# Sparse attention of a two-block network on one core: indexer and values first, selection cut by cost, heads of the first two query blocks as one unit, scores on half of the rows

## The chip, the core and the metric

The kernel runs on one core of a Trainium2 chip. The engines that matter are TensorE (PE in the profile; PEld is its weight load), VectorE (DVE), ScalarE (ACT), GpSimd (POOL) and SyncE (SP, which only issues DMAs here). The metric is the time of one execution on the device in microseconds (us). Before the change three runs took 2680.2, 2684.87 and 2683.86 us, with a median of 2683.86 us.

## What is computed

The network takes 512 tokens of one sequence through two blocks with fp32 weights. The change lies in the sparse attention of the second block. Cut to what matters:

```python
proj = h @ w_in                              # q 1024, k 256, v 256, qi 512, ki 64, wi 8 columns
q, k = _rope(_rmsnorm(q, ...)), _rope(_rmsnorm(k, ...))     # 16 heads, 4 key heads, 64 wide
qi, ki = _rope(qi), _rope(_layernorm(ki, ...))              # 8 index heads, one index key, 64 wide
wi = wi * (IDX_HEADS ** -0.5 * IDX_DIM ** -0.5)
topk = min(TOPK_MAX, T // 4)                 # 128 of 512 tokens
for each block of 128 queries:
    s = jnp.einsum('bqhd,bsd->bqhs', qib, ki)
    score = jnp.einsum('bqhs,bqh->bqs', jax.nn.relu(s), wib)
    score = jnp.where(causal, score, -jnp.inf)
    _, sel = lax.top_k(score, topk)
    logits = jnp.einsum('bqgrd,bqkgd->bqgrk', qg, kg) * scale   # only the selected, causal keys
    p = jax.nn.softmax(logits, axis=-1)
    o = jnp.einsum('bqgrk,bqkgd->bqgrd', p, vg)
return o @ w_out
```

## The kernel before

Activations lie transposed (features on partitions, 512 tokens on columns). A projection with fp32 weights is three products of a weight split in two parts: `whi` (a rounded copy that ACT makes, L124) and `wlo` (the rest, L126, a subtraction on DVE, or on POOL where `W.pool_lo` is set: every second one at True, all of them at 2). L461, L462 and L463 are those products. `one_T` computes one tile of 128 output features in 24 matmuls; behind each tile `proj_T` calls `step()`, which runs the closures in `deferred` and then one portion of the generator in `side_work`.

`dsa_block` works in this order: index projections (`ki`, then four tiles `QI`), two k tiles, eight q tiles, two v tiles, and then the attention. Index scores: `score()` (L1557) multiplies a QI tile, which holds two heads on the upper and lower 64 partitions, by `kiA` or `kiB`, copies of `ki` whose other 64 partitions are zero (POOL memsets, L1484 and L1485). ACT takes the relu (L1565) and DVE adds up the heads with their weights (L1567, L1569) into one row of scores for each query. Selection of block j: 16 rounds on DVE, each a search for the eight largest (`max`, L1589) and their replacement by a mark (`match_replace`, L1591), and then the mask `sel[j]` (`taken`, L1602). Block 0 has no more than 128 keys and takes the causal mask. The generator `select()` runs beside the k, q and v tiles: index scores a few heads at a time, rounds for blocks 1 and 2 by the table `PLAN`, then those for block 3.

The norm of q needs sums of squares: one L1628 matmul for each q tile adds to 20 rows in PSUM, and `sums_out` and `roots` make the factors `rq` from them once.

The attention is a loop over 32 units (j, hp), a unit being two heads of one query block: first blocks 1 and 2 in turn, then blocks 3 and 0 in turn. `scores(u)`: two matmuls L1730 against `KZ`, zero-padded copies of k; DVE masks, scales and takes the extreme in one instruction for each head (L1738); ACT takes the exponential with its row sum (L364). `divided(u)`, one unit later: reciprocal on DVE (L1746) and two POOL multiplications (L1748). `transposed(u)`, three units later: L1757 and two ACT copies (L1760). `values(u)`, five units later: L1770, with the two heads on the two halves of the columns, and a split of the result on ACT and DVE (L1774, L1775) for the output projection (L544).

What sets the order is the code itself: every engine takes its instructions in the order in which they are written.

Of the kernel before, what the change touches and what calls it, by code (L numbers as in the profile page):

```python
# [10 lines left out]
F32 = mybir.dt.float32  # L11
# [7 lines left out]
P = 128  # L19
# [218 lines left out]
def body(ctx: ExitStack, tc: tile.TileContext, A: dict, consts: bass.AP, out: bass.AP,  # L238
# [75 lines left out]
    mhalf = cp.tile([P, 4], F32, tag="mhalf", name="mhalf")  # L314
# [1138 lines left out]
    def dsa_block(layer):  # L1453
# [27 lines left out]
        kiA, kiB = big("U4"), big("U5")  # L1481
        KZ = [(big(f"U{6 + 2 * g}"), big(f"U{7 + 2 * g}")) for g in range(4)]
        def zeros(a, b):
            nc.gpsimd.memset(a[64:128], 0.0)  # L1484
            nc.gpsimd.memset(b[0:64], 0.0)  # L1485

        def evac_qi(c, ps):
            raw = tmp()
            nc.scalar.copy(raw, ps)
            rope(QI[c], raw)  # L1490
            zeros(*KZ[c])
# [4 lines left out]
        def evac_ki(c, ps):  # L1496
            raw = big("F4")
            nc.scalar.copy(raw[0:72], ps[0:72])
            zeros(kiA, kiB)
            x = raw[0:64]  # L1500

            def rest():
# [11 lines left out]
                def more():  # L1514
# [10 lines left out]
                    def last():  # L1525
                        nc.scalar.copy(kiA[0:64], x)
                        nc.scalar.copy(kiB[64:128], x)
# [18 lines left out]
        def score(*heads):  # L1546
# [3 lines left out]
            for j, h in heads:  # L1550
# [25 lines left out]
        PLAN = ((6, 0), (6, 0), (4, 4), (0, 4), (0, 4), (0, 4))  # L1576
        to_score = [(j, h) for j in (1, 2, 3) for h in (0, 2, 4, 6)]

        def select():

            def some_scores():
                if ready and to_score:
                    score(*[to_score.pop(0) for _ in range(min(2, len(to_score)))])

            def rounds(j, n):
                sc = marks[j][:, 0:P * (j + 1)]
                for _ in range(n):
                    m8 = colt((P, 8))
                    nc.vector.max(m8, sc)  # L1589
                    yield  # L1590
                    nc.vector.match_replace(sc, m8, sc, TAKEN)  # L1591
                    yield

            def some_rounds(*many):
                todo = [rounds(*x) for x in many if x[1]]
                while todo:
                    todo = [x for x in todo if next(x, True) is None]

            def taken(j):
                sel[j] = sel_t[:, j - 1] if j < 3 else sel_u[:, 0]  # L1600
                n = P * (j + 1)
                nc.vector.tensor_scalar(sel[j][:, 0:n], marks[j][:, 0:n], -2e38, NEG, op0=ALU.is_gt, op1=ALU.mult)  # L1602

            while len(to_score) > 8:
                some_scores()
                yield
            for n1, n2 in PLAN:
                some_rounds((1, n1), (2, n2))
                yield
                some_scores()  # L1610
            taken(1)
            taken(2)
            for _ in range(16):
                some_rounds((3, 1))
                yield
            taken(3)
# [5 lines left out]

        def squares(t, ps, start, stop):
            sq = side("acc", (P, S))
            nc.scalar.activation(sq, ps, AF.Square)

            def add():
                nc.tensor.matmul(ss[0:20, 0:S] if t >= 2 else ss[0:20, S:2 * S], zsel[:, t, :], sq,  # L1628
                                 start=start, stop=stop)

            deferred.append(add)

        kraw = [big("F5"), big("F0")]

        def evac_k(c, ps):
            nc.scalar.activation(kraw[c], ps, AF.Copy, scale=cB[:, 73:74])
            squares(c, ps, c == 0, c == 1)
            if c == 0:
                return

            def rest():
                v, y = tmp()[0:4], sp1.tile([P, 768], F32, tag="wide", name=nm("wide"))[0:4, 0:S]
                nc.vector.tensor_scalar(v, ss[0:4, S:2 * S], 1.0 / 64, EPS, op0=ALU.mult, op1=ALU.add)
# [4 lines left out]
                def copies(g):  # L1648
                    (a, b), o = KZ[g], kraw[g // 2][64 * (g % 2):64 * (g % 2) + 64]
                    nc.scalar.copy(a[0:64], o)  # L1650
                    nc.scalar.copy(b[64:128], o)
                    if g < 3:
                        deferred.append(lambda: copies(g + 1))

                def more():
                    for t in range(2):
                        p1 = pm()

                        nc.tensor.matmul(p1, kexp[t], y, start=True, stop=True)
                        o, z = kraw[t], side("ada_w", (P, 768))[:, 0:S]  # L1660
                        nc.vector.tensor_tensor(z, o, p1, op=ALU.mult)
                        rope(o, z, then=(lambda: copies(0)) if t else None)
# [270 lines left out]
```

## Time and profile before

| | us | busy share of the span |
|---|---|---|
| median of three runs | 2683.86 | |
| profiled execution | 2684.03 | |
| its span | 2682.3 | |
| PE busy | 2635.3 | 98% |
| DVE busy | 1385.7 | 52% |
| ACT busy | 918.2 | 34% |
| POOL busy | 541.9 | 20% |

The span is the time between the first and the last instruction of the profiled execution; 1.7 us lie around it. Busy shares are means over all stages. A stage is read by four views: the busy time in a stretch, the chain of work that ended last, the instructions of one engine in order of time with the idle time ahead of each and what ended it, and groups of like instructions with their mean.

### The profile page before, as it was taken

The numbers are of one execution on the slowest core, as the hardware profiler recorded it, in microseconds if no ns is written. First come the engines' busy times: TensorE is split into PE (matmuls) and PEld (weight loads), VectorE is DVE, ScalarE is ACT, GpSimd is POOL, SyncE is SP. The second block draws the span as 40 slices with busy tenths as digits, with TensorE's granted clock in tenths as the row PEclk, the third lists the DMA queues.
The fourth block names the chain that finished last, engine by engine and source line by source line (L and its number), as shares of the span: only waits on it lengthen the run. The fifth ranks groups of instructions, "written<-read, shape, count | busy, mean of one in ns | idle before, by whom it ended". The sixth has DMA issues, their size and how long they took to land.

```text
span 2682.3 us, 32412 instructions
## 1 busy us (share of the span) xinstructions
PE 2635.3 (98%) x12880; PEld 2174.9 (81%) x12880; DVE 1385.7 (52%) x2072; ACT 918.2 (34%) x1482; POOL 541.9 (20%) x548
## 2 busy tenths in 40 slices
PE   8999999999999999999999899999999999999999
PEld 7888889888777788888888766788888888888887
DVE  5545566375627454665555689453333544533332
ACT  4322233322344433423223436532222332322222
POOL 3211234154112211422123445220000200200000
PEclk9999999999999999999999899999999999999999
DMA  6555443223221323246545131032232322232322
GB/s 187 158 180 185 143 146 118 63 71 95 73 69 48 110 83 122 86 154 199 187 152 160 43 101 60 8 104 87 87 110 75 115 94 96 86 98 83 111 85 71
DMA packets 256474, 288.43 MB, mean 108 GB/s; under 512 B 9924, under 2 KB 238836, under 8 KB 256324
## 3 DMA queue, kind: packets, MB, share of 16 engines
q1 hardware_dynamic: 244196, 234.91, 28.0%
q0 software_dynamic: 10496, 50.95, 6.1%
q8 instruction: 101, 1.65, 0.3%
q10 hardware_dynamic: 1632, 0.52, 0.1%
q14 instruction: 49, 0.40, 0.0%
HBM read 278.59 MB, written 4.19 MB: 105 GB/s over the span
## 4 chain that ended last, share of the span: by engine, by line
PE 90%; DVE 7%; ACT 1%; issue 1%; POOL 1%; DMA 0%; SPq 0%; DVEq 0%; ACTq 0%; POOLq 0%
PE mm L461 25%; PE mm L462 25%; PE mm L463 25%; PE mm L544 2%; PE mm L657 1%; PE mm L659 1%; PE mm L658 1%; PE mm L1730 1%; PE B L1136 1%; DVE X L810 1%; DVE L L696 1%; PE mm L1770 1%; PE A L1279 1%; PE B L1302 1%; DVE F L1591 1%
## 5 line engine op out<-in xcount | busy, mean ns | idle before, releaser
L461 PE MATMUL mm<-H,whi 128*128 128x512 f32 (+1 forms) x2360 | 902.3, 382 | 0.0
L462 PE MATMUL mm<-L,whi 128*128 128x512 f32 (+1 forms) x2360 | 893.7, 379 | 1.4 <-DVE L L696 1.4
L463 PE MATMUL mm<-H,wlo 128*128 128x512 f32 (+1 forms) x2360 | 893.4, 379 | 0.9 <-DVE wlo L126 0.9
L126 DVE TENSOR_TENSOR wlo<-raw,whi 128x1024 fp32r<-128x1024 f32 (+3 forms) x431 | 505.9, 1174 | 555.0 <-ACT whi L124 550.8
L124 ACT CAST whi<-raw 128x1024 fp32r<-128x1024 f32 (+3 forms) x460 | 444.6, 968 | 411.4 <-PE mm L462 332.0
L461 PEld LDWEIGHTS mm<-H,whi 128*128 128x128 f32 x2360 | 445.5, 189 | 91.5 <-issue 10.6
L463 PEld LDWEIGHTS mm<-H,wlo 128*128 128x128 f32 x2360 | 445.3, 189 | 84.2 <-DVE wlo L126 1.6
L462 PEld LDWEIGHTS mm<-L,whi 128*128 128x128 f32 x2360 | 445.8, 189 | 83.6 <-DVE L L696 2.2
L461 PE MATMUL mm<-U,whi 128*128 128x512 f32 (+1 forms) x804 | 312.4, 389 | 0.0
L463 PE MATMUL mm<-U,wlo 128*128 128x512 f32 (+1 forms) x804 | 310.8, 387 | 0.0
L462 PE MATMUL mm<-U,whi 128*128 128x512 f32 (+1 forms) x804 | 310.7, 386 | 0.0
L413 POOL TENSOR_TENSOR acc<-acc,sq 128x512 f32<-128x512 f32 (+1 forms) x74 | 91.9, 1241 | 642.4 <-ACT sq L400 641.7
L670 ACT CAST U<-t 128x512 fp32r<-128x512 f32 x104 | 64.6, 621 | 406.9 <-POOL t L759 194.2
L461 PEld LDWEIGHTS mm<-U,whi 128*128 128x128 f32 x804 | 151.0, 188 | 33.5 <-issue 3.3
L463 PEld LDWEIGHTS mm<-U,wlo 128*128 128x128 f32 x804 | 151.0, 188 | 30.8
L462 PEld LDWEIGHTS mm<-U,whi 128*128 128x128 f32 x804 | 151.0, 188 | 30.2
L671 DVE TENSOR_TENSOR U<-t,U 128x512 fp32r<-128x512 f32 x104 | 72.1, 693 | 134.2 <-ACT U L670 134.2
L882 POOL DMA_DIRECT2D ada_w<-in_ada_w_dram x128 | 71.5, 558 | 281.6 <-DVE wide L906 220.5
L906 DVE SCALAR_TENSOR_TENSOR wide<-ada_w,csilu,wide 128x768 f32<-128x768 f32 x112 | 115.3, 1029 | 16.2 <-DMA ada_w<-in_ada_w_dram 16.2
L126 POOL TENSOR_TENSOR wlo<-raw,whi 128x1024 fp32r<-128x1024 f32 (+1 forms) x29 | 69.5, 2398 | 247.2 <-ACT whi L124 245.6
L757 DVE TENSOR_TENSOR t<-t,mm 128x512 f32<-128x512 f32 x88 | 60.3, 685 | 110.9 <-PE mm L463 110.8
L759 POOL TENSOR_TENSOR t<-t,R 128x512 f32<-128x512 f32 x44 | 56.4, 1283 | 218.4 <-DVE t L757 211.2
(386 smaller groups left out, 2791.7 us busy)
## 6 DMA issues: line engine op xcount, KB each, us to landing
ada_w<-in_ada_w_dram POOLq DMA_DIRECT2D x128, 384.0 KB, 3.6
raw<-in_ffn_w_up_dram SPq DMA_DIRECT2D x44, 1024.0 KB
raw<-in_ffn_w_gate_dram SPq DMA_DIRECT2D x43, 1024.0 KB
raw<-in_w_in_dram SPq DMA_DIRECT2D x30, 1024.0 KB
raw<-in_ffn_w_down_dram SPq DMA_DIRECT2D x32, 768.0 KB
raw<-in_ffn_w_down_dram SPq DMA_DIRECT2D x32, 640.0 KB
raw<-in_w_in_dram SPq DMA_DIRECT2D x24, 512.0 KB
raw<-in_conv_w_in_dram SPq DMA_DIRECT2D x12, 1024.0 KB
```

Of the source, the lines that this page charges most:

```text
L124: nc.scalar.copy(hi, raw)
L126: e.tensor_tensor(lo, raw, hi.bitcast(F32), op=ALU.subtract)
L413: (eng or nc.vector).tensor_tensor(self.acc[:, c], self.acc[:, c], sq[:, c], op=ALU.add)
L461: nc.tensor.matmul(ps, whi, hhi, start=start, stop=False)
L462: nc.tensor.matmul(ps, whi, hlo, start=False, stop=False)
L463: nc.tensor.matmul(ps, wlo, hhi, start=False, stop=stop)
L670: nc.scalar.copy(hi, src)
L671: nc.vector.tensor_tensor(lo, src, hi.bitcast(F32), op=ALU.subtract)
L757: nc.vector.tensor_tensor(s, s, ps, op=ALU.mult)
L759: nc.gpsimd.tensor_tensor(s, s, R, op=ALU.mult)
L882: nc.gpsimd.dma_start(loaded[i], A["ada_w_2"][layer, k * P:(k + 1) * P, 768 * cg:768 * (cg + 1)])
L906: nc.vector.scalar_tensor_tensor(acc, w, csilu[:, k:k + 1], acc, op0=ALU.mult, op1=ALU.add)
```

## The change

It touches `dsa_block` (with `plan_dsa`, the order in which weights are loaded, and the width of the constant `mhalf`).

- **Index.** `ki` is copied to both halves of one tile; a matmul of a head reads 64 partitions of `QI` and the same 64 of `ki`, so that the two heads of a tile stand on different halves of TensorE's rows. `kiA`, `kiB` and the memsets go. `score()` uses the tile `A` for every pair. All of block 1's index scores stand in one step.
- **Selection.** One generator takes block 1, 2 and 3 one after the other; `score()` of block j+1 stands between the rounds of block j. `select(much)` takes portions up to a cost.
- **q and k.** The v tiles stand ahead of the q tiles. v's weights are split by `W.pool_lo = True`, not 2. The squares of each q tile are summed by four small matmuls into columns, and `rq` of its two heads is made at once, with a DVE instruction and five POOL instructions. `KD` holds k doubled on both halves of a tile.
- **Units.** Eight units take blocks 0 and 1 of two heads together; they run beside the q tiles as far as these are there. Eight with block 2 and eight with block 3 follow. `divided(u)` is called right behind `scores(u)`. Results of the units beside the q tiles are kept in fp32 and split later.

The core of the diff (`HALF[i]` is rows 64*i to 64*i+64; line numbers of the changed kernel differ by up to some tens):

```diff
@@ plan_dsa
     plan.append(chunk_T("dsa", w, 0, ND, C["k"], 256))
+    plan.append(chunk_T("dsa", w, 0, ND, C["v"], 256))
     plan += [chunk_T("dsa", w, 0, ND, C["q"] + 256 * c, 256) for c in range(4)]
-    plan.append(chunk_T("dsa", w, 0, ND, C["v"], 256))
@@ score
-                    nc.tensor.matmul(ps, QI[h // 2][:, P * j:P * (j + 1)], (kiA, kiB)[i][:, 0:n],
-                                     start=True, stop=True)
+                for o in range(0, n, 256):
+                    for i in range(2):
+                        c = slice(o, min(o + 256, n))
+                        nc.tensor.matmul(parts[i - 2][2][:, c], QI[h // 2][HALF[i], P * j:P * (j + 1)], ki[HALF[i], c],
+                                         start=True, stop=True)
@@ selection
-        PLAN = ((6, 0), (6, 0), (4, 4), (0, 4), (0, 4), (0, 4))
+            for r in range(16):
+                m8 = colt((P, 8))
+                nc.vector.max(m8, sc)
+                nc.vector.match_replace(sc, m8, sc, TAKEN)
+                yield 0.3 + n / 470
+                if following and r % 4 == 1:
+                    score((following, r // 4 * 2))
+                    yield 0.5 + n / 400
...
+            for h in (0, 2, 4, 6):
+                score((1, h))
+                yield 1.0
+            for j in (1, 2, 3):
+                yield from rounds(j, j + 1 if j < 3 else None)
@@ evac_q
-            squares(2 + c, ps, c == 0, c == 7)
+            sq = side("acc", (P, S))
+            nc.scalar.activation(sq, ps, AF.Square)
             rope(Q[c], raw)
+            def add():
+                both = pm()
+                for j in range(NT):
+                    nc.tensor.matmul(both[:, 2 * j:2 * j + 2], sq[:, P * j:P * (j + 1)], zsel[:, 2, 4:6], start=True,
+                                     stop=True)
+                v, y, z = colt((P, 8)), colt((P, 8)), colt((P, 8))
+                nc.vector.tensor_scalar(v, both[:, 0:8], 1.0 / 64, EPS, op0=ALU.mult, op1=ALU.add)
+                nc.gpsimd.tensor_tensor(y, v, mhalf, op=ALU.pow)
...
+                nc.gpsimd.tensor_tensor(z, y, y, op=ALU.mult)
+                nc.gpsimd.tensor_tensor(z, z, v, op=ALU.mult)
+                nc.gpsimd.tensor_scalar(z, z, 0.5 / 8.0, -1.5 / 8.0, op0=ALU.mult, op1=ALU.add)
...
-        W.pool_lo = 2
-        proj_T("dsa", 2, H, evac_v)
@@ units
-        units = [(j, hp) for hp in range(8) for j in (1, 2)] + [(j, hp) for hp in range(8) for j in (3, 0)]
+        units = [((0, 1), hp) for hp in range(8)] + [((2,), hp) for hp in range(8)] + [((3,), hp) for hp in range(8)]
...
+                for c in range(0, n, 256):
+                    w = min(256, n - c)
+                    for i in range(2):
+                        nc.tensor.matmul(pss[i][:, o + c:o + c + w], Q[hp][HALF[i], P * j:P * (j + 1)],
+                                         KD[hp // 2][HALF[i], c:c + w], start=True, stop=True)
...
+        def unit_step(turn, value):
+            if at[2] < at[1] and at[0] - at[2] >= value:
+                values(at[2])
+                at[2] += 1
+            if at[1] < len(units) and at[0] - at[1] >= turn:
+                transposed(at[1])
+                at[1] += 1
+            u = at[0]
             if u < len(units):
-                while sel[units[u][0]] is None:
-                    step()
                 scores(u)
+                divided(u)
+            at[0] += 1
+        def beside_q():
+            while True:
+                u = at[0]
+                if sel[1] is not None and u < 8 and there[0] > u + 2:
+                    unit_step(1, 2)
+                    select(3.0)
+                else:
+                    select(5.5)
+                yield
+        side_work.append(beside_q())
+        W.pool_lo = True
+        proj_T("dsa", 2, H, evac_k)
+        proj_T("dsa", 2, H, evac_v)
+        proj_T("dsa", 8, H, evac_q)
...
+        while at[2] < len(units):
+            if at[0] < len(units):
+                while sel[units[at[0]][0][-1]] is None:
+                    select(2.0)
+            unit_step(3, 5)
...
+            select(1.4)
             step()
```

How the instructions stand now, at three places. First TensorE behind the second k tile (`A` and `mm` are PSUM tiles, the `U` tiles are QI and ki, `whi` and `H` belong to the next projected tile). Before:

```order
L1628 MATMUL B_11369<-acc_11400,dsa_consts 20x512
L1557 MATMUL A_11436<-U_1184_10974,U_1180_10970 128x256
L1557 MATMUL A_11436<-U_1185_10975,U_1180_10970 128x256
L1557 MATMUL mm_11439<-U_1184_10974,U_1181_10971 128x256
L1557 MATMUL mm_11441<-U_1185_10975,U_1181_10971 128x256
L461 MATMUL mm_11474<-H_1149_10885,whi_11317 128x512
```

and of the changed kernel:

```order
L1650 MATMUL B_11354<-acc_11396,dsa_consts 20x512
L1559 MATMUL A_11432<-U_1184_10974,U_1180_10970 128x256 x2
L1559 MATMUL A_11441<-U_1184_10974,U_1181_10971 128x256 x2
L1559 MATMUL A_11450<-U_1184_10974,U_1182_10972 128x256 x2
L1559 MATMUL A_11459<-U_1184_10974,U_1183_10973 128x256 x2
L461 MATMUL mm_11484<-H_1149_10885,whi_11304 128x512
```

The four heads of the last two QI tiles (`U_1182`, `U_1183`), which stood behind the next tile, stand ahead of it, and all pairs write the one tile `A`.

Second DVE at one unit (`t` are the probabilities, `col` the extremes and the row sums, `F` the row of scores under selection). A unit of block 2 before:

```order
L1738 ISA t_12209,col_12210<-mm_12204,U_1227_11367,R_11473 128x384
L1738 ISA col_12210 128x1
L1738 ISA t_12213,col_12214<-mm_12206,U_1227_11367,R_11473 128x384
L1738 ISA col_12214 128x1
L1589 MAX col_12217<-F_1324_11826 128x8
L1591 MATCH_REPLACE F_1324_11826<-col_12217,F_1324_11826 128x512
L1746 RECIPROCAL col_12208<-col_12208 128x2
```

and the first unit of blocks 0 and 1 in the changed kernel, where L1730, L1739, L1584 and L1585 are what L1738, L1746, L1589 and L1591 were:

```order
L1730 ISA t_11940,col_11942<-mm_11934,masks,R_11365 128x128
L1730 ISA col_11942 128x1
L1730 ISA t_11941,col_11942<-mm_11935,masks,R_11365 128x128
L1730 ISA col_11942 128x1
L1730 ISA t_11940,col_11942<-mm_11934,U_1222_11352,R_11365 128x256
L1730 ISA col_11942 128x1
L1730 ISA t_11941,col_11942<-mm_11935,U_1222_11352,R_11365 128x256
L1730 ISA col_11942 128x1
L1739 RECIPROCAL col_11943<-col_11943 128x4
L1584 MAX col_11957<-F_1258_11510 128x8
L1585 MATCH_REPLACE F_1258_11510<-col_11957,F_1258_11510 128x384
```

The round that stood between a unit's last reduction and its reciprocal stands behind the reciprocal.

Third POOL beside one q tile (`U` is the q tile that is rotated, `ada_w` its raw copy, `t` the swapped halves, `wlo` the low part of a weight). Before:

```order
L1466 TENSOR_TENSOR U_1249_11467<-ada_w_11940,rc_8270 128x512
L126 TENSOR_TENSOR wlo_11951<-raw_11536,whi_11950 128x1024
L1469 TENSOR_TENSOR t_11944<-t_11944,rs_8271 128x512
L1466 TENSOR_TENSOR U_1250_11468<-ada_w_11996,rc_8270 128x512
L1469 TENSOR_TENSOR t_12000<-t_12000,rs_8271 128x512
```

and of the changed kernel:

```order
L1675 TENSOR_TENSOR col_11926<-col_11925,mhalf 128x8
L1677 TENSOR_TENSOR col_11927<-col_11926 128x8
L1678 TENSOR_TENSOR col_11927<-col_11927,col_11925 128x8
L1679 TENSOR_SCALAR col_11927<-col_11927 128x8
L1680 TENSOR_TENSOR R_11365<-col_11927,col_11926 128x4x2
L1741 TENSOR_SCALAR t_11940<-t_11940,col_11943 128x128
L1741 TENSOR_SCALAR t_11941<-t_11941,col_11943 128x128
L1741 TENSOR_SCALAR t_11940<-t_11940,col_11943 128x256
L1741 TENSOR_SCALAR t_11941<-t_11941,col_11943 128x256
L1466 TENSOR_TENSOR U_1230_11360<-ada_w_11974,rc_8270 128x512
L126 TENSOR_TENSOR wlo_11985<-raw_11551,whi_11984 128x1024
L1469 TENSOR_TENSOR t_11978<-t_11978,rs_8271 128x512
```

Between two rotations POOL now has the five instructions of `rq` and the four multiplications of a unit.

## Rows read from the trace of the kernel before

**Rows 1.** Busy time of the engines in four stretches of the sparse attention: start and end, length, then the busy time (and instructions) of PE, PEld, DVE, ACT and POOL, TensorE's granted clock, the DMA engines' share and GB/s. The first stretch holds the k, q and v tiles but for the last; the last ends where the output projection begins.

```profile
1531.80:1630.40 98.60, 91.36 (x333) 59.65 (x332) 82.42 (x156) 42.59 (x71) 51.66 (x38) 0.97 0.36 107
1630.40:1649.30 18.90, 16.16 (x89) 10.36 (x87) 17.79 (x61) 13.01 (x42) 7.49 (x11) 0.91 0.18 57
1649.30:1671.40 22.10, 22.06 (x158) 14.46 (x160) 19.24 (x73) 17.59 (x63) 9.76 (x18) 1.00 0.00 1
1671.40:1717.30 45.90, 45.84 (x373) 30.75 (x373) 23.92 (x106) 36.69 (x128) 18.82 (x36) 1.00 0.01 2
```

**Rows 2.** The chain of work that ended last, in order of time (start, length, engine, tile and line, instructions), where it passes from DVE to PE, in a unit of block 2, in units of block 3, and at the start of the output projection.

```profile
1648.33 0.76 DVE F L1591 x2
...
1649.34 1.56 PE mm L1730 x4
1650.90 0.81 PE mm L1770 x12
1651.70 0.81 PE B L1757 x6
...
1673.01 1.72 PE mm L1730 x4
...
1689.58 1.02 PE mm L1770 x16
1690.60 1.03 PE A L1757 x8
...
1717.30 0.43 PE mm L544 x2
```

**Rows 3.** DVE in order of time: start, length, line, operation, tile and shape, and in brackets the idle time before it with what ended it. The start of the selection; a unit of block 1 and its neighbours in the stretch beside block 3's rounds; a unit of block 2; the mask of block 3.

```profile
1552.55 2.81 DVE L1569 SCALAR_TENSOR_TENSOR F<-sq,wcol,F 128x256 f32<-128x256 f32 x4 [2.96 <-ACT sq L1565]
1556.70 1.39 DVE L126 TENSOR_TENSOR wlo<-raw,whi 128x1024 fp32r<-128x1024 f32 x1 [1.33 <-ACT whi L124]
1558.01 0.41 DVE L1589 MAX8 col<-F 128x8 f32<-128x256 f32 x1
...
1634.36 0.47 DVE L1738 CUSTOM_DVE_ANT_0 acc<-mm,U,R 128x256 f32<-128x256 f32 x1
...
1635.16 0.69 DVE L1589 MAX8 col<-F 128x8 f32<-128x512 f32 x1
...
1636.55 0.15 DVE L1746 RECIPROCAL col<-col 128x2 f32<-128x2 f32 x1
1636.63 0.60 DVE L1738 CUSTOM_DVE_ANT_0 t<-mm,U,R 128x384 f32<-128x384 f32 x1
...
1637.83 0.69 DVE L1589 MAX8 col<-F 128x8 f32<-128x512 f32 x1
...
1656.65 0.28 DVE L1775 TENSOR_TENSOR L<-mm,H 128x128 fp32r<-128x128 f32 x1
1656.84 0.16 DVE L1746 RECIPROCAL col<-col 128x2 f32<-128x2 f32 x1
...
1657.98 0.08 DVE L1738 DVE_READ_ACCUMULATOR2_ANT col<- 128x1 f32 x1
...
1665.62 0.42 DVE L1602 TENSOR_SCALAR U<-F 128x512 bf16<-128x512 f32 x1
```

**Rows 4.** The reductions of block 0's units over the whole span, one group of like instructions (count, busy us, mean ns of one, idle time before them).

```profile
L1738 DVE CUSTOM_DVE_ANT_0 t<-mm,masks,R 128x128 f32<-128x128 f32 x16 | 5.3, 347 | 0.1
```

**Rows 5.** ACT in order of time: the exponentials of the unit of block 2 whose second reduction is read out at 1657.98 us in rows 3; the last row is the read of the second row sum.

```profile
1657.64 0.61 ACT L364 ACTIVATE t<-t,col 128x384 f32<-128x384 f32 x1 [0.81 <-DVE col L1738]
...
1658.76 0.19 ACT L364 ACTIVATION_READ_ACCUMULATOR t<-t,col 128x1 f32 x1
```

**Rows 6.** PE in order of time. First, from an earlier stage, two matmuls with a contraction over four rows, L1257 on rows 0 to 3 of the array and L1258 on rows 32 to 35; then the four scores of a unit of block 1 and the first products with the values behind them.

```profile
757.27 0.59 PE L1257 MATMUL A<-rc,cst 4*128 4x512 f32 x1
757.27 0.59 PE L1258 MATMUL A<-rc,cst 4*128 4x512 f32 x1
...
1652.35 1.03 PE L1730 MATMUL mm<-U,U 128*128 128x256 f32 x4
1653.31 0.32 PE L1770 MATMUL mm<-wide,F 128*64 128x128 f32 x1
...
1653.47 0.27 PE L1770 MATMUL mm<-wide,F 128*64 128x128 f32 x1
...
1653.58 0.27 PE L1770 MATMUL mm<-wide,F 128*64 128x128 f32 x1
```

**Rows 7.** The same two DVE instructions, the last step of a rotation (L1472) and the low part of a weight (L126), with POOL at work and without, in order of time.

```profile
1528.16 1.75 DVE L1472 TENSOR_TENSOR U<-U,t 128x512 f32<-128x512 f32 x1 [2.43 <-POOL t L1469]
1531.57 3.79 DVE L126 TENSOR_TENSOR wlo<-raw,whi 128x1024 fp32r<-128x1024 f32 x1 [1.66 <-ACT whi L124]
1535.88 0.67 DVE L1472 TENSOR_TENSOR U<-U,t 128x512 f32<-128x512 f32 x1
...
1542.98 1.21 DVE L126 TENSOR_TENSOR wlo<-raw,whi 128x1024 fp32r<-128x1024 f32 x1
```

**Rows 8.** POOL: in order of time, what it did while the slow L126 of rows 7 ran; then groups of like instructions over the whole span, a power of two columns (L435) and a unit's multiplication (L1748).

```profile
1530.49 2.54 POOL L1469 TENSOR_TENSOR t<-t,rs 64x512 f32<-64x512 f32 x2
...
L435 POOL TENSOR_TENSOR col<-col,mhalf 128x2 f32<-128x2 f32 x14 | 9.8, 703 | 25.1 <-DVE col L433 25.1
L1748 POOL TENSOR_SCALAR t<-t,col 128x128 f32<-128x128 f32 x16 | 5.8, 376 | 5.8 <-DVE col L1746 4.6 <-ACT H L1774 0.8 <-PE mm L1730 0.4
```

More of the change, by code (lines that the diff above doesn't have):

```diff
@@ L1574, in score @@
                                             compare_op=ALU.is_ge, fill=NEG)
-        PLAN = ((6, 0), (6, 0), (4, 4), (0, 4), (0, 4), (0, 4))
[L1577 to L1616, printed above, removed]
@@ new lines, in selection, with select @@
+        def selection():
+            while not ready:
+                yield 100.0
+            for h in (0, 2, 4, 6):
[3 more added lines that the diff above has]
+                yield from rounds(j, j + 1 if j < 3 else None)
+        selecting = selection()
+        def select(much):
+            while much > 0:
+                cost = next(selecting, None)
+                if cost is None:
+                    break
+                much -= cost
@@ L1636, in evac_k, with copies, more @@
             nc.scalar.activation(kraw[c], ps, AF.Copy, scale=cB[:, 73:74])
-            squares(c, ps, c == 0, c == 1)
-            if c == 0:
-                return
+            sq = side("acc", (P, S))
+            nc.scalar.activation(sq, ps, AF.Square)
+            def copies(g):
+                o = kraw[g // 2][HALF[g % 2]]
+                for i in range(2):
+                    nc.scalar.copy(KD[g][HALF[i]], o)
+                if g < 3:
+                    deferred.append(lambda: copies(g + 1))
+            def more(y):
+                for t in range(2):
+                    p1 = pm()
+                    nc.tensor.matmul(p1, kexp[t], y, start=True, stop=True)
+                    o, z = kraw[t], side("ada_w", (P, 768))[:, 0:S]
+                    nc.vector.tensor_tensor(z, o, p1, op=ALU.mult)
+                    rope(o, z, then=(lambda: copies(0)) if t else None)
             def rest():
                 v, y = tmp()[0:4], sp1.tile([P, 768], F32, tag="wide", name=nm("wide"))[0:4, 0:S]
-                nc.vector.tensor_scalar(v, ss[0:4, S:2 * S], 1.0 / 64, EPS, op0=ALU.mult, op1=ALU.add)
+                nc.vector.tensor_scalar(v, ss[0:4, 0:S], 1.0 / 64, EPS, op0=ALU.mult, op1=ALU.add)
                 act(y, v, AF.Ln)
@@ L1646, in rest @@
                 newton(y, v, 1.0, tmp()[0:4])
[L1648 to L1662, printed above, removed]
-                deferred.append(more)
-            deferred.append(lambda: deferred.append(lambda: deferred.append(rest)))
-        side_work.append(select())
-        W.pool_lo = True
-        proj_T("dsa", 2, H, evac_k)
+                deferred.append(lambda: more(y))
+            def add():
+                nc.tensor.matmul(ss[0:20, 0:S], zsel[:, c, :], sq, start=c == 0, stop=c == 1)
+                if c:
+                    deferred.append(rest)
+            deferred.append(add)
         Q = [big(f"U{14 + i}") for i in range(8)]
+        there = [0]
+        rq = big("R", F32, (P, NT, 16))
         def evac_q(c, ps):
@@ L1777, in dsa_block @@
-        for u in range(len(units) + 5):
-            if 0 <= u - 5:
-                values(u - 5)
-            if 0 <= u - 3 < len(units):
-                transposed(u - 3)
-            if 0 <= u - 1 < len(units):
-                divided(u - 1)
+            for x, (j, o) in enumerate(places(js)):
+                for b in range(j + 1):
+                    for i in range(2):
+                        nc.tensor.matmul(ob[64 * i:64 * i + 64, P * x:P * (x + 1)],
+                                         V[b // 2][:, 256 * (b % 2) + 64 * kv:256 * (b % 2) + 64 * kv + 64],
+                                         pts[i][:, o + P * b:o + P * (b + 1)], start=(b == 0), stop=(b == j))
@@ new lines, in dsa_block @@
+        n = at[0]
+        while at[1] < n:
+            transposed(at[1])
+            at[1] += 1
+            step()
+        while at[2] < n:
+            values(at[2])
+            at[2] += 1
+            step()
+        phase[0] = False
+        waiting = list(range(n))
+        while at[2] < len(units):
[3 more added lines that the diff above has]
+            unit_step(3, 5)
+            if waiting:
+                hp = waiting.pop(0)
+                parted(hp, slice(0, 256), kept[hp // 2][:, hp % 2])
+            select(1.4)
```

139 lines of the change are left out of this document (69 added, 70 removed).

## The prediction, made before the changed kernel ran

> **What bounds the kernel now.** I read the stretches first, then the chain, then one engine at a time. Over the whole span PE is 98% busy, but that is a mean: in the sparse attention the stretches differ [rows 1]. While the k, q and v tiles run, PE is busy 91.36 us of 98.60 and DVE 82.42; in the next 18.90 us PE is busy 16.16 and DVE 17.79; from 1649.3 to 1717.3 us PE is practically full. The chain says the same: up to 1649 us it runs through DVE's rounds (L1589 and L1591), from 1649.34 through PE alone until the output projection starts at 1717.30 [rows 2]. In order of time DVE starts the rounds at 1558.01 us and writes the last mask at 1665.62 [rows 3]. So the stage has two bounds in series: a DVE stream of 107.6 us, which nobody can shorten without taking work from DVE, and what PE still has to do behind it, now 1717.30 - 1665.62 = 51.7 us. I therefore forecast the time of the last mask (T) and PE's rest behind it, and add them.
>
> **The DVE stream, part by part.** The rounds themselves are the same 48. What moves T is the rest.
>
> *Start.* Ahead of the first round DVE idles 2.96 us for index scores and 1.33 us for a weight [rows 3]. The change puts all of block 1's scores ahead of the next tile, so up to 4.3 us could be won. Against it, four pairs now share one PSUM tile and PE stands in front of each until ACT has read the one before, which holds up the next projected tile and its weights by up to 3 us. I take -1, with -4.3 and +3 as ends.
>
> *Reciprocals.* This is the largest term. Before, a round stood between a unit's last reduction and its reciprocal: the unit at 1634.36 us is read out by 1635.16, one round runs, and the reciprocal takes its place at 1636.55 without idling [rows 3]. After, it stands right behind the last reduction, and DVE takes nothing else until ACT's exponentials have their row sums. A unit of block 2 shows what that is: the last reduction is read out at 1657.98 + 0.08 = 1658.06, the second row sum at 1658.76 + 0.19 = 1658.95 [rows 3, 5], so 0.89 us, and 0.95 with the hand-over. Queued behind it on DVE are rounds, index sums and the low parts of weights for which PE waits. By the code's budgets eleven units (eight of blocks 0 and 1, three of block 2) stand ahead of the last mask: 11 x 0.95 = 10.4 us. The lower end is 0 (DVE would have waited there anyway); the upper is 8 x 1.5 + 3 x 0.95 = 14.9, where a unit of two blocks with four exponentials waits 1.5 us, an estimate from two exponentials in 1658.95 - 1657.64 = 1.31 us.
>
> *Low parts of v's weights.* Two of them come from POOL to DVE, at 1.21 us without POOL at work and 3.79 with it [rows 7]: +2.4 to +7.6, I take 3, since the clean row is the nearer one.
>
> *Reductions.* Before T stood seven units of block 1 at 1635.16 - 1634.36 = 0.80 us and six of block 2 at 1637.83 - 1636.63 = 1.20: 12.8 us [rows 3]. Now eight of both small blocks at 0.80 + 2 x 0.27 = 1.34 (0.347 less the 0.08 that consecutive ones overlap [rows 4]) and three at 1.20: 14.4. That is +1.6. Splits of results (0.2 us apart at 1656.65 [rows 3]) become fewer but wider: +0.4.
>
> *POOL.* The factors of q cost five POOL instructions for each q tile, and the units beside the q tiles add four multiplications of 0.38 us and more. The trace has powers of two columns only, 0.70 us [rows 8]; at that price the five are 3.5 us, at a third of it 1.1; I take 2.5. POOL is busy 51.66 of 98.60 us there [rows 1], so it holds 8 x 2.5 = 20 more. They are off the path, but DVE's instructions with two inputs slow down beside POOL: L1472 takes 1.75 us against 0.67, L126 3.79 against 1.21 [rows 7]. The ten memsets that go stood with the index projections, ahead of the stream. I take +3, ends 0 and +15.5 (six steps with one slow L126 more, 2.58 each).
>
> T moves by -1 + 10.4 + 3 + 1.6 + 0.4 + 3 = +17.4 us, to 1683.0. The DVE instruction for the factors of q replaces the block of them at the end and costs nothing; the doubled k takes the same eight ACT copies as the padded one.
>
> **PE's rest behind T.** Left there are five scores, eight transposes and ten value products of block 2 and eight of each of block 3. With row tiles a pair of scores should take half: the earlier stage has two matmuls on different rows that start together at 757.27 us and both take 0.59 [rows 6]. From the chain [rows 2]: scores 5 x 1.56 / 2 + 8 x 1.72 / 2 = 10.8, transposes 8 x 0.81 + 8 x 1.03 = 14.7, values 10 x 0.81 + 8 x 1.02 = 16.3, in all 41.8, less about 1 that PE does while T comes: 41. Before it was 51.7, so 10.7 us are won here. The units that ran behind T before and now run beside the q tiles are part of that.
>
> The scores' halving ahead of T is worth nothing by this reading: PE then waits for DVE. What it would be worth if PE set the pace: the units save 8 x (0.96 + 1.56 + 1.72 + 0.52) / 2 = 19 us [rows 2, 6] (0.52, block 0, is a third of block 2's 1.56), and the index scores, with half as many heads and no block 0, about 8.5, an estimate. PE's 175.4 busy us of the four stretches [rows 1] would become 148 and the stage could end 37 us earlier, if nothing waited. I keep this as the floor, 2647.
>
> A switch of how the array is divided costs PE little in the trace: behind L1730, the first pair of L1770 takes 1653.47 - 1653.31 = 0.16 us, the next 0.11 [rows 6]. The Trainium skill, "TensorEngine Tiling (Array Packing)", section "Tiling Modes", has a rule that speaks against the change: changing the mode drains TensorE. By the row, one more switch in each of the 13 units behind T is 0.7 us; by a whole drain of about one matmul's 0.3 us (an estimate from the length of L1770) it is 4, and the time would be 2695 instead of 2691.
>
> **Sum.** +17.4 - 10.7 = +6.7 us: the output projection starts at 1724.0 instead of 1717.30. Behind it nothing changes. The profiled execution took 2684.03 us (span 2682.3 and 1.7 around it), 0.17 over the median, so the forecast is 2691.
>
> **Rivals.**
>
> *The waits of the reciprocals are covered (faster).* Place: the eleven reciprocals. If DVE has slack at them because PE or ACT is late anyway, and POOL's work hides, T moves by only 17.4 - 10.4 - 3 = +4 and the stage ends 6.7 us earlier: 2677. It decides from where DVE idles over 7 us in all for other reasons. For it: DVE was busy 82.42 of 98.60 us beside the tiles [rows 1]. Against it: in the next stretch, where the rounds of block 3 run, it was busy 17.79 of 18.90 [rows 1], and the idle times of rows 3 lie ahead of the first round.
>
> *POOL paces the q steps (slower).* If each of eight q tiles holds a rotation for 1.08 us more (8.6), or six hold a low part for 2.58 (15.5), T moves 6 to 12 beyond the 3 in my sum: 2700. During the slow L126 at 1531.57 POOL was at work without a gap from 1530.49 [rows 7, 8]. The Trainium skill, "SBUF — State Buffer", section "SBUF: two separate sides", says why it could: DVE and GpSimd share a port pair as an exclusive lock, held for a whole instruction, and the loser blocks. The trace agrees in kind: 3.79 us against 1.21.
>
> *Row tiles don't run side by side.* The change would not do what it says: scores cost PE what they did, 10.8 us more behind T: 2702. The rows at 757.27 speak against it, though they are four rows high, not 64.
>
> **How the numbers follow.** A measurement of this kernel tells 0.2% (5.4 us) from no change. Forecast 0.48, of it 0.30 above 2689.3 and 0.18 below; waits covered 0.28, of it 0.23 faster than 2678.5 and 0.05 not; POOL 0.16, of it 0.15 slower; row tiles alone 0.06; the rest, a stage that PE sets, 0.02 faster. So faster 0.25, same 0.24, slower 0.51. The range reaches from 2668, some 9 us below the covered case, to 2704, which takes in the POOL case and the row tiles; its own range without the rivals is 2684 to 2699. About 0.18 lie outside.
>
> **What would show it.** Right: DVE's reciprocals with idle time of about 1 us ahead, ended by the row sum on ACT; the last mask near 1683; pairs of scores that start together; PE idle beside the q tiles and full behind the last mask, with some 41 us left. Wrong: the last mask before 1672 with PE full beside the q tiles (then PE's savings count and the time falls), or POOL busy without gaps beside the q tiles and L126 at over 2.5 us (then it is the second rival).

## The result and the profile after

The changed kernel takes 2697.76 us (median of four runs, 2696.67 to 2699.45) against 2682.94 on the same chip: 1.0057 times the time, with an interval of 1.0039 to 1.0074, so about 15 us slower. The forecast was 2691, slower by 7. The profiled execution took 2697.28 us (span 2695.6).

First the chain of work that ended last, of the changed kernel, as in [rows 2] (L1720 are the scores, L1767 the values, L1750 the transposes):

```profile
1684.05 0.75 DVE F L1585 x2
1684.81 0.34 DVE L L671
1685.15 0.04 issue
1685.19 2.18 PE mm L1720 x6
1687.37 1.48 PE mm L1767 x12
1688.85 1.47 PE B L1750 x6
1690.32 1.58 PE mm L1720 x8
...
1693.53 0.85 PE mm L1720 x8
...
1715.17 1.06 PE mm L1720 x8
1716.23 1.02 PE mm L1767 x16
1717.26 1.02 PE B L1750 x8
...
1730.91 9.19 PE mm L544 x75
```

It has the shape that was forecast: DVE's rounds, then TensorE alone. The output projection starts at 1730.91 instead of 1717.30. A pair of scores takes 0.85 and 1.06 us where it took 1.56 and 1.72 [rows 2], so the two heads do run side by side. The first rows behind DVE take 2.18, 1.48 and 1.47 us; why, the stretches show, with the columns of [rows 1]:

```profile
1531.80:1630.40 98.60, 82.26 (x405) 61.52 (x404) 74.62 (x172) 46.88 (x99) 53.80 (x61) 0.90 0.30 89
1630.40:1660.00 29.60, 24.19 (x160) 19.10 (x158) 22.16 (x59) 14.00 (x42) 26.94 (x37) 0.83 0.32 97
1660.00:1690.00 30.00, 20.36 (x97) 15.15 (x97) 24.37 (x74) 12.39 (x42) 8.07 (x15) 0.52 0.00 1
1690.00:1720.00 30.00, 30.00 (x300) 22.85 (x300) 18.77 (x67) 26.65 (x77) 13.48 (x22) 0.97 0.01 2
```

From 1660 to 1690 us TensorE was busy 20.36 of 30 us at a granted clock of 0.52, close to the lower of its two levels (1.2 GHz), and DVE 24.37. The clock is still there for the first rows behind DVE: twelve values took 1.48 us and six transposes 1.47, against 0.81 for the same counts before [rows 2]. DVE is less busy than before in the first stretch too, 74.62 against 82.42. Where its time went, DVE in order of time shows (L1584 and L1585 are the rounds, L1730 the reductions, L1739 the reciprocal; idle time and its end in brackets):

```profile
1551.70 0.43 DVE L1584 MAX8 col<-F 128x8 f32<-128x256 f32 x1 [0.40 <-POOL F L1574]
...
1558.88 0.42 DVE L1568 TENSOR_SCALAR F<-sq,wcol 128x384 f32<-128x384 f32 x1 [5.25 <-ACT sq L1566]
...
1634.83 0.35 DVE L1730 CUSTOM_DVE_ANT_0 t<-mm,masks,R 128x128 f32<-128x128 f32 x1 [1.89 <-PE mm L1720]
...
1636.18 0.09 DVE L1730 DVE_READ_ACCUMULATOR2_ANT col<- 128x1 f32 x1
1637.19 0.18 DVE L1739 RECIPROCAL col<-col 128x4 f32<-128x4 f32 x1 [0.93 <-ACT t L364]
...
1688.76 0.43 DVE L1591 TENSOR_SCALAR U<-F 128x512 bf16<-128x512 f32 x1
```

and as groups of like instructions between the first round and the last mask (columns as in [rows 4], and behind the idle time what ended it):

```profile
L1472 DVE TENSOR_TENSOR U<-U,t 128x512 f32<-128x512 f32 x8 | 10.0, 1247 | 1.1 <-POOL t L1469 1.1
L1730 DVE CUSTOM_DVE_ANT_0 t<-mm,masks,R 128x128 f32<-128x128 f32 x14 | 4.3, 347 | 4.6 <-PE mm L1720 4.6
L1472 DVE TENSOR_TENSOR F<-F,t 128x512 f32<-128x512 f32 x2 | 4.1, 2074 | 0.0
L1739 DVE RECIPROCAL col<-col 128x4 f32<-128x4 f32 x8 | 1.4, 178 | 7.4 <-ACT t L364 6.4 <-ACT sq L364 1.0
L1674 DVE TENSOR_SCALAR col<-mm 128x8 f32<-128x8 f32 x8 | 1.3, 157 | 1.0 <-PE mm L1671 1.0
L1739 DVE RECIPROCAL col<-col 128x2 f32<-128x2 f32 x3 | 0.5, 166 | 2.9 <-ACT sq L364 1.9 <-ACT t L364 1.0
L1568 DVE TENSOR_SCALAR F<-sq,wcol 128x384 f32<-128x384 f32 x1 | 0.4, 420 | 5.2 <-ACT sq L1566 5.2
```

Eleven reciprocals wait 7.4 + 2.9 = 10.3 us for ACT's row sums; 5.2 us go to the first index scores of block 2, 4.6 to scores that TensorE has not made yet, 1.0 to its sums of squares, 1.1 to rotations on POOL.

One thing has to be set right before traces are compared. The stage doesn't start at the same time in every execution. ACT in order of time, the copy of the projected `ki`, ahead of which nothing of the attention stands, in the kernel before and the changed one:

```profile
1512.13 0.58 ACT L1498 COPY F<-mm 72x512 f32<-72x512 f32 x1 [2.52 <-PE mm L463]
```

```profile
1510.28 0.58 ACT L1497 COPY F<-mm 72x512 f32<-72x512 f32 x1 [2.52 <-PE mm L463]
```

Over all profiles it lies between 1505.70 and 1512.77 us, with no order by kernel. So distances from this copy are compared: before, the first round came 45.9 us behind it, the last mask 153.5, the output projection 205.1; after, 41.4, 178.5 and 220.6. The stage grew by 15.5 us, which is the measured difference within the spread of the runs.

The first round is earlier and the tile behind it late, which the trace shows too. Block 1's four pairs of index scores share the tile `A`, and TensorE stood in front of it for 0.76, 5.00 and 0.76 us. In the longest of these ACT's relu had nowhere to write until DVE's first sum (L1568), and that sum stood behind a rotation for which DVE waited until POOL was done (PE, ACT and DVE in order of time, of the changed kernel):

```profile
1546.55 1.22 PE L1559 MATMUL A<-U,U 64*128 64x256 f32 x4 [5.00 <-ACT sq L1566]
1545.58 0.39 ACT L1566 ACTIVATE sq<-A 128x256 f32<-128x256 f32 x1 [5.30 <-DVE F L1568]
1544.53 0.69 DVE L1472 TENSOR_TENSOR U<-U,t 128x512 f32<-128x512 f32 x1 [2.88 <-POOL t L1469]
1549.69 0.79 PE L461 MATMUL mm<-H,whi 128*128 128x512 f32 x1
```

The next projected tile (the last row) starts at 1549.69 us, and the index scores of block 2, behind it, are what DVE waits for at 1558.88. TensorE had idled 3.84 us ahead of these scores as well, and from 1538.3 on the clock was at its lower level for 13.7 us; this stretch, and the one at the same distance from the copy in the kernel before:

```profile
1538.30:1552.00 13.70, 7.18 (x23) 3.85 (x23) 7.51 (x12) 4.29 (x11) 3.22 (x4) 0.50 0.50 163
```

```profile
1540.15:1553.85 13.70, 13.68 (x49) 9.14 (x48) 6.48 (x9) 4.91 (x11) 7.04 (x6) 0.88 0.53 169
```

### The profile page after: what moved, and what is told of

It reads as the page before. It is cut to its first block, busy times and chain, and to the rows that moved or that the text cites. A ratio compares the mean times of both kernels' runs of the same rounds, so it can differ in the third digit from the quotient of the medians.

```text
span 2695.6 us, 32613 instructions
## 1 busy us (share of the span) xinstructions
PE 2627.8 (97%) x13020; PEld 2186.6 (81%) x13020; DVE 1387.5 (51%) x2060; ACT 918.2 (34%) x1460; POOL 558.6 (21%) x577
## 5 line engine op out<-in xcount | busy, mean ns | idle before, releaser
L126 DVE TENSOR_TENSOR wlo<-raw,whi 128x1024 fp32r<-128x1024 f32 (+3 forms) x432 | 503.1, 1165 | 551.4 <-ACT whi L124 547.5
L126 POOL TENSOR_TENSOR wlo<-raw,whi 128x1024 fp32r<-128x1024 f32 (+1 forms) x28 | 66.5, 2375 | 253.3 <-ACT whi L124 249.6
```

Of the source, the lines that this page charges most:

```text
L126: e.tensor_tensor(lo, raw, hi.bitcast(F32), op=ALU.subtract)
```

## The experiments

Distances from the copy of `ki` in the profiled execution, and the measured times, each with the ratio to the kernel before on the same chip and its interval. The runs come from several chips, on which the kernel before took 2681.62 to 2682.99 us, so medians of different rows compare to about 1 us; each distance is that of one execution.

| kernel | last mask | output projection | median us | ratio |
|---|---|---|---|---|
| before | 153.5 | 205.1 | 2682.94 | |
| after | 178.5 | 220.6 | 2697.76 | 1.0057 (1.0039 to 1.0074) |
| e1_round_between | 170.5 | 214.0 | 2691.82 | 1.0034 (1.0022 to 1.0047) |
| e2_no_power | 179.1 | 220.9 | 2698.03 | 1.0053 (1.0038 to 1.0068) |
| e4_four_heads_a_step | 176.5 | 219.4 | 2694.47 | 1.0048 (1.0034 to 1.0062) |
| e5_before_row_tiles | 152.9 | 202.2 | 2678.54 | 0.9986 (0.9977 to 0.9995) |
| e6_no_units_beside_q | 141.7 | 207.4 | 2686.02 | 1.0011 (1.0002 to 1.0019) |
| e7_scores_first | 174.7 | 217.8 | 2695.16 | 1.0051 (1.0035 to 1.0066) |
| e8_scores_first_start | 166.0 | 217.1 | 2693.55 | 1.0044 (1.0030 to 1.0057) |
| e9_before_rows_start | 151.9 | 205.9 | 2683.08 | 1.0003 (0.9994 to 1.0012) |
| e10_fewer_rounds_beside_q | 158.3 | 208.4 | 2685.70 | 1.0012 (1.0003 to 1.0021) |
| e11_fewer_rounds_power_on_act | 158.0 | 210.6 | 2688.13 | 1.0022 (1.0011 to 1.0032) |
| e12_before_rows_scores_first | 161.6 | 212.1 | 2690.94 | 1.0035 (1.0022 to 1.0047) |
| e13_before_rows_low_on_pool | 152.4 | 201.8 | 2678.78 | 0.9990 (0.9980 to 0.9999) |

**The reciprocals.**

```diff
                 scores(u)
+                select(1.0)
                 divided(u)
...
-                    select(3.0)
+                    select(1.9)
...
-            select(1.4)
+            select(1.0)
```

> The changed kernel, but one round of the selection stands between a unit's reductions and its reciprocal again (the rounds behind the unit are one fewer, so their number for each unit stays). DVE theory (the waits of the eleven reciprocals, 0.94 us each in the profile after, lie on the stream that sets the last mask): the waits go, the last mask comes some 10 us earlier than 1688.8, and the time falls from 2697.8 by 7 to 11 us, to about 2688. Rival, coupling with TensorE (DVE would wait for the next scores or projected tile instead): the time falls by less than 3 us, and DVE's idle time shows up ahead of the reductions.

The mask came 8.0 us earlier, the output projection 6.6, the median is 6 lower, a little short of the 7 to 11 that were expected. In e1's groups the reciprocals idle no more, but DVE waits longer for TensorE and for POOL's part of the rotations, and so not all of the 10.3 us came back:

```profile
L1472 DVE TENSOR_TENSOR U<-U,t 128x512 f32<-128x512 f32 x8 | 8.4, 1047 | 3.4 <-POOL t L1469 3.4
L1730 DVE CUSTOM_DVE_ANT_0 t<-mm,masks,R 128x128 f32<-128x128 f32 x14 | 4.3, 346 | 5.5 <-PE mm L1720 5.5
L1739 DVE RECIPROCAL col<-col 128x4 f32<-128x4 f32 x8 | 1.3, 168 | 0.0
L1674 DVE TENSOR_SCALAR col<-mm 128x8 f32<-128x8 f32 x8 | 1.2, 156 | 2.2 <-PE mm L1671 2.2
```

**POOL's power.** `op=ALU.pow` becomes `op=ALU.mult`; the norm of q is left out.

> The changed kernel with the power of 128x8 on POOL (L1675, 1.64 us each, eight of them) replaced by a multiplication; the norm of q is left out by that. POOL theory (POOL's instructions for the factors of q pace the q tiles): some 11 us of POOL go and the time falls by 6 to 12 us. DVE theory: only the slowed DVE instructions beside it recover, up to 3 us.

POOL's instruction fell from 1.66 us to 0.23, and neither the mask, the output projection nor the time came earlier. In this execution DVE waited 6.7 us for the first index scores of block 2, not 5.2, so a gain of 1 or 2 us could be hidden; the 6 to 12 us of the POOL theory could not. The rival of a POOL that paces the q steps had foretold 2700, near the time measured, but its cause isn't there.

**Block 1's scores in more PSUM tiles.** `score((1, h))` for four h becomes `score((1, h), (1, h + 2))` for two.

> The changed kernel, but the index scores of block 1 come as two calls of four heads, so that the second pair of each call writes two tiles of the mm pool and not the one tile A. If the wait for A at the start sets the last mask, the first round starts 1 to 3 us earlier and the time falls as much. DVE theory: DVE idles 5.25 us two rounds later anyway, for the scores of block 2 behind the next tile, so the time falls by under 1 us.

The first round came 1.8 us earlier, the next scores idled DVE 5.6 us instead of 5.25, and the stage is 1.2 us shorter, which the times don't tell from none. TensorE stood 3.3 us for the rotation on DVE here too, so the one tile `A` was not what held it most.

**Row tiles alone**, in the kernel before:

```diff
...
-                nc.tensor.matmul(ps[:, 0:n], Q[hp][:, P * j:n], KZ[hp // 2][i][:, 0:n], start=True, stop=True)
+            for c in range(0, n, 256):
+                w = min(256, n - c)
+                for i in range(2):
+                    nc.tensor.matmul(pss[i][:, c:c + w], Q[hp][HALF[i], P * j:n], KD[hp // 2][HALF[i], c:c + w],
+                                     start=True, stop=True)
```

(and the same in `score`, with `ki` and `KD` as in the change and without `kiA`, `kiB`, `KZ` and the memsets).

> The kernel before with the row tiles alone: index scores and attention scores on the two halves of the rows, k and ki doubled, no memsets; order, units and norms as before. DVE theory: the mask of block 3 stays near 1665 us, and behind it the scores save 8 x (1.72 + 0.45) / 2 plus one of block 2, some 9.5 us; up to 14 us if the backlog of TensorE from 1649 on shrinks too: 2669 to 2673.5 against 2682.9. Rival, the row tiles are what costs (drains between modes, lower clock): no gain, or a loss.

Faster than the kernel before, and so than both, by 4 us (interval 1 to 6), not by 9 to 13. The mask stayed where it was, as expected; behind it only 2.3 us went (51.6 to 49.3). The chain of this kernel shows why:

```profile
1682.67 0.47 PE mm L1732 x4
1683.16 0.19 ACT sq L364
1683.35 0.16 ACT H L1776
1683.53 0.30 DVE L L1777
1683.88 1.46 PE mm L1732 x8
```

TensorE is no longer alone in it. A pair of block 3 takes 1.46 us, not 1.06. It starts at 1683.88, when DVE's split (L1777) has freed the first of its PSUM tiles, and that split stands behind ACT's exponentials and copy. The first head's matmuls then run alone until 1684.20: the second tile is freed by DVE's reduction of block 0's unit, which stands behind the split and is read out here (DVE in order of time):

```profile
1684.07 0.08 DVE L1740 DVE_READ_ACCUMULATOR2_ANT col<- 128x1 f32 x1
```

So of the 0.66 us that a pair of block 3 saves in the changed kernel (1.72 to 1.06), 0.40 turned into waits for buffers. The pairs of block 0, which the expectation halved too, take 0.47 us in the first row above, no less than in the kernel before:

```profile
1681.29 0.45 PE mm L1730 x4
```

**No units beside the q tiles**, on top of e1: `beside_q` holds only `select(5.5)`.

> As e1_round_between, but no unit runs beside the q tiles: the selection alone does, and all 24 units follow behind the tiles. Coupling theory (units beside the tiles shorten nothing on DVE and make DVE and TensorE wait for each other): DVE's idle time for scores (5.5 us) and sums of squares (2.2) goes, the q tiles end earlier, and TensorE has 24 units of about 2.4, 2.5 and 3.1 us behind them, some 64 us from about 1640: the output projection starts near 1705 to 1710 instead of 1723, the time is 2673 to 2681. Rival (the units beside the tiles are what the order earns): five units of 2.4 us come back behind the mask, 12 us more than e1, 2700 or above.

The output projection came 6.6 us earlier than in e1 and the median fell by 5.8: the coupling is there. DVE's 5.5 + 2.2 + 3.4 us of idle time in e1's groups are 0 here. The edit also lets more rounds stand beside each tile, so that the mask comes 28.8 us earlier and more of the units lie behind it. The last product of the tiles ended 116.9 us behind the copy of `ki`, 13.1 us earlier than in e1, as expected. But the gain stopped at 2686, short of the forecast of 2673 to 2681, because TensorE then ran ahead of DVE: its first scores waited 6.89 and 6.21 us for PSUM tiles that DVE's step of the factors of q (L1674) frees, and that step stands behind four rounds and a rotation each time (PE in order of time):

```profile
1638.67 0.79 PE L1720 MATMUL mm<-U,U 64*128 64x128 f32 x2 [6.89 <-DVE col L1674]
1645.67 3.00 PE L1720 MATMUL mm<-U,U 64*128 64x128 f32 x14 [6.21 <-DVE col L1674]
```

The output projection started at 1718.98; without these 13.1 us it would have been 1705.9, an estimate, and in the range that was expected. The stretch behind the last products, of e6 and then of e10, where fewer rounds stand beside the tiles (`select(4.0)`):

```profile
1635.00:1650.00 15.00, 3.99 (x17) 2.93 (x17) 14.62 (x37) 1.86 (x8) 12.51 (x17) 0.50 0.23 75
```

```profile
1635.00:1650.00 15.00, 9.39 (x42) 6.00 (x42) 13.13 (x46) 6.32 (x26) 11.79 (x21) 0.53 0.21 70
```

> As e6_no_units_beside_q, with a budget of 4.0 instead of 5.5 for the selection beside each projected tile, so that more rounds stand among the units. DVE theory: beside the tiles DVE is the bound (busy 14.4 of 15 us in e6 while TensorE fell to 4 of 15 from 1635 to 1650), so the tiles end some 10 us earlier, about 12 rounds move among the units, where TensorE is the bound, and the output projection starts 6 to 12 us earlier than in e6: 2674 to 2680. Rival (POOL paces the q tiles in e6, its factors of q and rotations): the tiles end less than 4 us earlier and the time falls by less than 3 us.

> As e10_fewer_rounds_beside_q, with the power of 128x8 taken by ACT as logarithm and exponential (the Newton step on POOL stays). If POOL's 1.64 us for each power hold up the rotations and so the tiles once DVE has room, the time falls by 2 to 6 us more than e10; if they lie beside other work, it stays within 1 us of e10, or rises because ACT waits for DVE's sum.

In e10 TensorE works 5.4 us more in that stretch: its waits for L1674 fall from 13.1 to 5.8 us. But the tiles' products end only 3.5 us earlier, not 10, its waits for POOL's multiplications (L1741) rise from 2.0 to 5.1 us, and the rounds moved behind the tiles take the rest back (the mask is 16.5 us later). In e11, which takes `y` by `AF.Ln` and `AF.Exp`, those waits for POOL fall to 0.7 us, but ACT's logarithm stands waiting for L1674, and TensorE waits 6.3 us for ACT's squares behind it (0.5 in e10): the median is 2.4 us higher, as the expectation allowed. So e11 moved a wait and doesn't tell what POOL's power alone costs. Neither beats e6.

**Order within a step**, on top of e1: `scores(u)` first, then the values and transposes of earlier units; e8 also counts block 1's scores at 0.3 and asks `r % 4 == 3`.

> As e1_round_between, but TensorE takes a unit's scores ahead of the values and transposes of the units before it. If DVE's 5.5 us of idle time ahead of the reductions come from that order, they fall under 2 us and the time falls by 3 to 5 us from 2691.8. Rival: the scores are late because the projected tile ahead of them is; then nothing changes.

> As e7_scores_first, with more rounds of block 1 ahead of the first index scores of block 2 (the step that holds block 1's scores counts them at 0.3 each, and block 2's scores stand behind every fourth round, not every second one of four). DVE theory: the 5.3 us of idle time after the first two rounds shrink to 2 or less, and the last mask and the end come 3 us earlier than in e7. Rival: block 2's scores come later and DVE waits for them there; no change.

e7 made it worse by 3.8 us in the stage, which neither side expected: DVE's wait ahead of the reductions moved to transposes (3.3 us, ended by L1750, and 3.1 by scores). In e8 the idle time at the start fell from 5.35 to 0.6 us and the mask came 8.7 us earlier than in e7, but the end only 0.7: rounds that are done early leave more units behind the mask. The mask alone doesn't set the end; rounds and units together do.

**The start, in the kernel before.** e5 with all index scores of block 1 in one step and the first rounds right behind.

> As e5_before_row_tiles, with all index scores of block 1 in one step and the rounds of the first portion right behind. DVE theory: the rounds start some 5 us earlier and the last mask comes 3 to 6 us earlier than 1658.6; TensorE sets the end there in part, so the time falls by 1 to 4 us from 2678.5. Rival (TensorE, not DVE, sets the end in that kernel): no change.

The first round came 5.6 us earlier than in e5, the mask 1.0, and the output projection 3.6 later; the median is 4.5 higher, where 1 to 4 less were expected. DVE idled 10.9 us on the way to the mask, against 2.8.

**Two tries at a better version**, both from e5: the scores first in each unit, and `W.pool_lo = 2` for k, q and v.

> As e5_before_row_tiles, with a unit's scores on TensorE ahead of the values and transposes of earlier units. In e5 a pair of block 3 took 1.46 us instead of the 1.06 of the changed kernel, and the chain shows why: the second of its PSUM tiles was held by the result of the unit before until DVE's split (L1777). If that wait is what halves the gain, the scores come down to about 1.1 us and the time falls by 8 x 0.35 = 3 us from 2678.5. Rival: the wait moves to the values or the transposes behind; no change.

> As e5_before_row_tiles, with all low parts of the k, q and v weights on POOL (2 instead of True). DVE theory: the stream of 107.7 us up to the last mask loses three instructions of 5.7 us in all, the mask comes 4 to 6 us earlier, the time falls by 2 to 5 us from 2678.5. Rival (POOL's 2.4 us for each are late for TensorE, and slow DVE's rotations down): no change or up to 4 us more.

The split holds the first PSUM tile of the pair, not the second as the expectation has it. e12's pair of block 3 did fall to 1.11 us, but the stage grew by 10 us and the median by 12: the split (L1777) now stands behind the exponentials of a later unit, and DVE idles 8.2 us ahead of it. e13 changed nothing. The stream up to the mask was 107.4 us against 107.7: the three low parts gone from DVE (3.4 us in e5, at 1.22 each, not the 5.7 that the expectation took from the kernel before) came back as other DVE instructions slowed beside POOL, such as the mask of block 1, in e5 and in e13:

```profile
L1601 DVE TENSOR_SCALAR U<-F 128x256 bf16<-128x256 f32 x1 | 1.4, 1380 | 0.0
```

```profile
L1601 DVE TENSOR_SCALAR U<-F 128x256 bf16<-128x256 f32 x1 | 2.5, 2484 | 0.0
```

## Why the prediction was right, and where it was short

The direction and the mechanism hold, but the size was less than half of what was measured: DVE's stream sets the stage up to the last mask, the reciprocals' waits are its largest new term, and TensorE's rest behind the mask shrinks. Step by step, with elapsed times from DVE's rows between the first round and the mask (from start to start, less idle time):

| term | forecast | measured |
|---|---|---|
| start | -1 | 41.4 - 45.9 + 5.25 = +0.8 |
| reciprocals | +10.4 | +10.35 |
| low parts | +3 | 5.9 - 5.7 = +0.3 |
| reductions | +1.6 (its own rows add up to +1.5) | 14.0 - 11.9 = +2.1 |
| splits | +0.4 | 2.0 - 1.6 = +0.5 |
| POOL beside DVE | +3 | rotations 13.5 - 9.7 = +3.8, sums of index scores 11.0 - 12.0 = -1.0 |
| waits for TensorE and rotations | none | 4.6 + 1.0 + 1.1 = +6.7 |
| last mask | +17.4 | +25.0 |
| TensorE's rest | 41 (-10.7) | 42.1 (-9.5) |
| stage | +6.7 | +15.5 |

The remaining 1.5 us of the mask are small rows: longer reads and reciprocals, rounds that overlap less with their neighbours, and the new instruction for the factors (0.9), which does cost no more than the block that it replaced.

The step that failed is the sum of the DVE stream. It took DVE as a list of instructions that runs without gaps, as it did before, and priced one new wait. But a unit beside a q tile makes DVE wait for scores that TensorE has only after 24 products, values and transposes, and TensorE wait for DVE in turn. PE in order of time, at the next projected tile, whose PSUM tile DVE's step of the factors of q (L1674) frees only behind rounds, a low part and a rotation:

```profile
1606.29 0.57 PE L461 MATMUL mm<-H,whi 128*128 128x512 f32 x1 [4.23 <-DVE col L1674]
```

In e6, without these units, no projected tile waits so. The profile of before could not show it, since no unit ran there. That these units, with the fewer rounds beside them, cost and don't earn is shown by e6. The end of +3 us for the start was too low as well: TensorE stood 6.5 us in front of `A`. The term for the low parts was wrong in its base: of the three of before two were slow ones beside POOL (1.22, 2.30 and 2.37 us), the five of after nearly clean (1.22 to 1.36).

That TensorE's rest came out at 42.1 us, near 41, is in part luck. In the chain the 13 pairs of scores took 14.8 us, not 10.8: a pair takes 1.06 or 0.85 us where half would be 0.86 or 0.78, and the first two, at the lower clock, took 2.18 and 1.58. Against it TensorE did 3.6 us of the work ahead of the mask, not 1. The prediction has no term for the clock. The four rows up to 1691.90 took 3.4 us more than like rows behind them (0.85, 0.81, 0.80, 0.85); what the lower clock cost ahead of the mask, no run separates. Whether the 0.2 us over half of a pair come from the switch of the array's division is open too.

Of the 15.5 us, e1 shows 6.6 for the place of the reciprocals and e6 another 6.6 for the units beside the q tiles (with the rounds that took their place). e9, in the order of before, shows 3.6 for block 1's scores in one step. The row tiles give back 2.9 (e5). If these add, which no run tests, they are 13.9 together: e9 and e5 are changes to another order, e5's gain was held back by a wait that the changed kernel doesn't have, and whether the start costs the same in the changed order e4 and e8 did not tell. The rest is open.

The covered-waits rival fell with e1, though some of the 10.3 us were covered: the mask gained 8.0 and the stage 6.6. The POOL rival fell with e2 and with low parts that stayed at 1.22 to 1.36 us; its slower rotations did come, with 3.8 of the 8.6 us that it named. The row-tile rival fell with the scores' 1.06 us.

## What to carry to other kernels

A consumer put right behind its producer on another engine waited 0.86 to 0.99 us here, eleven times; one piece of independent work between them took these waits away, and 6.6 of the 10.3 us came off the stage. Before work is moved beside other work, ask whether the engine that bounds the stage gets a gap from it: units beside the tiles took nothing from DVE and gave it waits. And when a matmul gets shorter, look at who frees its PSUM tile: in e5 0.40 of the 0.66 us that a pair could save went into that.

## What the runs showed that was not expected

The start of the same stage shifts by up to 7 us from one execution to the next, as much as the times of one kernel spread (2674.7 to 2681.7 in e5); distances from a common instruction told kernels apart where times from the span's start did not. DVE's mask of block 1 (L1601), with one input and bf16 out, took 0.28 us in e9 and 2.48 beside POOL in e13, so not only instructions with two tensor inputs suffer. The Trainium skill, "SBUF — State Buffer", section "SBUF: two separate sides", has it so: beside two inputs it names DVE's modes that use both ports. Whether the mask runs in one, no run shows. And the index sums took 11.0 us after, 12.0 before, though POOL was busier in the first stretch (53.80 us against 51.66); why, no run shows.
